# Expert gates of a decoder step scattered by matmuls: three bfloat16 parts in place of one float32 product, scaled on VectorE

## The chip, the core and the metric

The kernel runs on one core of a Trainium2 chip. The core has engines that run side by side and wait for each other by semaphores: TensorE (PE in the rows; PEld is its weight load), VectorE (DVE), ScalarE (ACT), GpSimd (POOL) and SyncE (SP). Each works through its own instructions in the order in which they stand. TensorE reads its operands from the on-chip memory SBUF and adds up its products in PSUM. The metric is the device time of one execution in microseconds; lower is better.

## The reference, cut to what matters

One step of a decoder layer: differential attention and a gated linear attention side by side, cross attention, and last a feed-forward layer of 16384 single-neuron experts, of which each token uses 128 (8 heads times 16). The change lies in that layer.

```
def one(xt):
    ...
    top_s, j = lax.top_k(cand_s, PEER_TOPK)
    e = jnp.take_along_axis(cand_i, j, axis=-1).reshape(blk, -1)
    g = jax.nn.softmax(top_s, axis=-1).reshape(blk, -1)
    act = jax.nn.gelu(jnp.einsum('ted,td->te', u[e], xt).astype(jnp.float32))
    return jnp.einsum('te,ted->td', (g * act).astype(xt.dtype), v[e])
```

There are 1024 prompt tokens (tiles 0 to 7 of 128) and 64 sample tokens (tile S). `e` is the expert's number, `g` its gate.

## The kernel before, in words

**Two ways to the experts.** For some tokens (`GORDER`) the kernel fetches the rows of `u` and `v` that they chose, one indirect DMA on POOL for each of 128 places (line 1232), and DVE makes a dot product (line 1238) or an accumulation (line 1245) of each: 640 of either. For the other 448 tokens (`DENSE`: half of tile 2 and tiles 3, 4, 5) it computes all 16384 experts with matmuls (`dense`, lines 1303 to 1370) and multiplies by a gate that is zero where an expert wasn't chosen. That needs the gates of a token as a 128 by 128 matrix W, where expert `e` stands in row `e >> 7` and column `e & 127`.

**How W is made.** `gates` (lines 1262 to 1301) runs once for each of the four tiles. It loads `e` and `g`, takes `e` apart, and transposes all three on TensorE, so that a token is a column and its 128 choices lie on the partitions. Then it goes through the tokens in 14 groups of 32 and, within a group, four times 8 tokens, 56 steps in all. In a step DVE compares a table of numbers `io8` with the row numbers of 8 tokens (`oa`, line 1288) and with their column numbers (`eb`, line 1289): one-hot rows, 128 wide, with the 8 tokens innermost. ACT multiplies `eb` by the gates, token by token (`ob`, 8 instructions, line 1291). TensorE forms `oa` transposed times `ob` for each token (line 1295), which adds each gate into its place; `oa` and `ob` are float32 here, and the operands of one token are 8 elements apart in memory. The profile shows a float32 matmul as two instructions. ACT copies the sums out of PSUM (line 1297), and SP stores a group to `Wd` in DRAM (line 1300). `oa`, `eb` and `ob` have two buffers each.

**What runs beside it.** `drive` (line 1481) steps the last post pass (tiles 6 and 7: output projection, cross attention, expert query, expert selection) and `gates` in turns, by the costs that they yield. In the rows, the post pass's matmuls are `accP` (lines 286 to 288), its weight splitting is `ws` (272 on ACT, 273 on DVE), and its selections are many small DVE instructions (lines 1014 to 1072, among them `eq`, line 1052, and `oh`, line 1055). A gather step is let in between (`paced`, line 1447). Its instructions are queued behind the instruction that `gmark` names on that instruction's engine; `gates` sets `gmark` to its scalings.

**What sets the order.** A scheduler with a timeline of its own orders the instructions of each engine, within the dependences and priorities. The dense stage follows: it loads `xs`, transposes it to `xTd` (lines 1310, 264, 246), then runs over blocks of 8 times 128 experts: scores `S` (line 1323), gelu and multiplication by W (`hx`, lines 1327 to 1334, which give `H`), and output `po` (line 1353).

Of the kernel before, what the change touches and what calls it, by code (L numbers as in the profile page):

```python
# [7 lines left out]
F32 = mybir.dt.float32  # L8
F32R = mybir.dt.float32r
BF = mybir.dt.bfloat16  # L10
I32 = mybir.dt.int32
U32 = mybir.dt.uint32
AF = mybir.ActivationFunctionType
OP = mybir.AluOpType
AX = mybir.AxisListType

P = 128
# [88 lines left out]
def step_kernel(ctx: ExitStack, tc: tile.TileContext, consts, a, outs):  # L106
    nc = tc.nc
# [3 lines left out]
    def mkpool(name, side="left"):  # L111
        return tc.tile_pool(name=name, bufs=1, side=side, reuse_waits="tile")
# [15 lines left out]
    def bank(tag):  # L128
        pool, n = banks[tag]
        return pool.tile([P, 512], F32, tag=tag, name=tag, bufs=n)  # L130
# [1131 lines left out]
    def gates(wp, t, io8):  # L1262

        e = wp.tile([P, P], I32, tag="we", name="we", bufs=1)
        nc.sync.dma_start(out=e, in_=eD[t * P:(t + 1) * P])
        ab = wp.tile([P, 2, P], I32, tag="wab", name="wab", bufs=1)
        nc.vector.tensor_scalar(ab[:, 0], e, 7, None, op0=OP.logical_shift_right)
        nc.vector.tensor_scalar(ab[:, 1], e, 127, None, op0=OP.bitwise_and)
        abg = wp.tile([P, 3, P], F32, tag="wf", name="wf", bufs=1)
        nc.vector.tensor_copy(abg[:, :2], ab)  # L1270
        nc.sync.dma_start(out=abg[:, 2], in_=gD[t * P:(t + 1) * P])
        pt = bank("wb").rearrange("p (j n) -> p j n", n=P)
        for j in range(3):
            nc.tensor.transpose(out=pt[:, j], in_=abg[:, j], identity=ident)
        T = wp.tile([P, 2, P], BF, tag="wT", name="wT", bufs=2)
        nc.vector.tensor_copy(T, pt[:, :2])
        tg = wp.tile([P, P], F32, tag="wm", name="wm", bufs=2)
        nc.vector.tensor_copy(tg, pt[:, 2])
        for g in range(4):
            if (t, g) not in goff:  # L1280
                continue
            st = wp.tile([P, 32, 4, 32], F32, tag="wst", name="wst", bufs=2)
            for q in range(4):
                c = slice(32 * g + 8 * q, 32 * g + 8 * q + 8)
                oa = wp.tile([P, P, 8], F32, tag="woa", name="woa", bufs=2)
                eb = wp.tile([P, P, 8], BF, tag="web", name="web", bufs=2)
                ob = wp.tile([P, P, 8], F32, tag="wob", name="wob", bufs=2)
                nc.vector.tensor_tensor(oa, io8, T[:, 0, c].unsqueeze(1).broadcast_to([P, P, 8]), op=OP.is_equal)
                nc.vector.tensor_tensor(eb, io8, T[:, 1, c].unsqueeze(1).broadcast_to([P, P, 8]), op=OP.is_equal)
                for k in range(8):  # L1290
                    gmark[0] = nc.scalar.activation(ob[:, :, k], eb[:, :, k], AF.Copy, scale=tg[:, c.start + k:c.start + k + 1]).ins
                for q4 in range(2):
                    ps = bank("wb").rearrange("p (t b) -> p t b", b=P)
                    for k in range(4):
                        nc.tensor.matmul(ps[:, k], lhsT=oa[:, :, 4 * q4 + k], rhs=ob[:, :, 4 * q4 + k], start=True, stop=True)  # L1295
                    o = 8 * q + 4 * q4
                    nc.scalar.copy(st[:, :, :, o:o + 4].rearrange("p g b t -> p (g b) t"),  # L1297
                                   ps.rearrange("p t b -> p b t"))
                yield 2.5
            nc.sync.dma_start(out=Wd[:, :, goff[t, g]].rearrange("g a x -> a g x"),  # L1300
                              in_=st.rearrange("p g b t -> p g (b t)"))
# [150 lines left out]
    gmark = [None]  # L1452
# [69 lines left out]
    op = ops.enter_context(mkpool("omg"))  # L1522
# [10 lines left out]
    while True:  # L1533
        c = next(m2)
# [31 lines left out]
    def all_gates(ts):  # L1566
        for t, _, _ in ts:
            yield from gates(gp, t, io8)
# [48 lines left out]
```

## Time and profile before

| | us |
|---|---|
| median of three runs | 4846.96 |
| lowest and highest of them | 4844.46 and 4854.68 |
| the profiled execution | 4846.62 |
| its span, first to last instruction | 4844.8 |

The profile is of one execution. Its busy time is a union of an engine's instructions; the same engine can be the limit in one stretch and idle in the next, so the stretches are to be read one by one. A wait is put down to what ended it. The granted clock of TensorE is a share of its full 2.4 GHz. The stages here, in us from the span's start: one-hot stage with post pass from 2975 to 3290, the rest of the post pass's selections up to about 3463, the dense stage's start beside and behind them, and the dense stage proper from about 3600 to the end.

### The profile page before, as it was taken

The page shows a single profiled execution, that of the slowest core. Times are in us where ns is not written, and L with a number is a line of the kernel's source. Part 1 is how long each engine was busy: PE and PEld are TensorE (multiplying, and loading weights), DVE is VectorE, ACT ScalarE, POOL GpSimd, SP SyncE. Part 2 cuts the span into 40 slices and gives each one's busy share as a digit, 9 for nine tenths or more (in the row PEclk, how much of TensorE's full clock was granted, in tenths as well). Part 3 has the DMA queues.
Part 4 walks back from the last instruction along what each step waited for, and adds up shares of the span by engine and source line. Part 5 has one row for each costly group of instructions (what it writes and reads, how often), then busy time and mean ns, then how long its engine had stood idle before and what let it go on. Part 6 is the DMA issues. An engine that isn't in the chain of part 4 may idle for free.

```text
span 4844.8 us, 74087 instructions
## 1 busy us (share of the span) xinstructions
PE 4003.1 (83%) x23952; PEld 3106.8 (64%) x23952; DVE 3626.2 (75%) x7813; ACT 2188.8 (45%) x4874; POOL 1742.3 (36%) x1509
## 2 busy tenths in 40 slices
PE   7987999789886776378678537997289999999999
PEld 5654666455554454256345326896279999999998
DVE  4442336766766789978778998679888889888887
ACT  4565666556652534155433336993123323332332
POOL 2000000124334545345444534233345444444542
PEclk9999999899998888589889768897699999999999
DMA  6778888799998887588788657787789999999996
GB/s 187 245 249 272 308 285 293 252 326 350 347 342 287 290 271 247 168 276 282 267 281 282 205 161 240 253 262 256 233 303 343 350 328 345 336 340 332 338 346 237
DMA packets 574629, 1370.40 MB, mean 283 GB/s; under 512 B 66401, under 2 KB 131233, under 8 KB 573473
## 3 DMA queue, kind: packets, MB, share of 16 engines
q1 hardware_dynamic: 376128, 669.92, 40.9%
q0 software_dynamic: 184320, 671.17, 40.6%
q10 hardware_dynamic: 13792, 24.58, 1.4%
q8 instruction: 190, 3.11, 0.3%
q14 instruction: 199, 1.62, 0.1%
HBM read 1306.52 MB, written 58.39 MB: 282 GB/s over the span
## 4 chain that ended last, share of the span: by engine, by line
PE 47%; DMA 18%; DVE 17%; issue 7%; ACT 5%; POOL 3%; SPq 2%; DVEq 0%; ACTq 0%; POOLq 0%
PE po L1353 11%; PE S L1323 11%; DMA g<-in_peer_v,e 7%; DVE g L1238 4%; PE tk L761 3%; DMA kp<-in_cache_diff_k 3%; DVE acc L1245 3%; PE wb L1295 3%; PE pt L264 2%; DMA g<-in_peer_u,e 2%; PE acc L287 2%; PE acc L286 2%; PE acc L288 2%; PE px L806 2%; PE pS L767 2%
## 5 line engine op out<-in xcount | busy, mean ns | idle before, releaser
L1232 POOL DMA_INDIRECT g<-in_peer_u,e x640 | 757.0, 1183 | 1086.4 <-DVE dots L1238 705.8
L1232 POOL DMA_INDIRECT g<-in_peer_v,e x640 | 756.1, 1181 | 927.7 <-DVE acc L1245 563.8
L1245 DVE SCALAR_TENSOR_TENSOR acc<-g,dots,acc 128x1024 f32<-128x1024 f32 x640 | 820.2, 1282 | 143.8 <-DMA g<-in_peer_v,e 140.1
L1238 DVE CUSTOM_DVE_ANT_0 g<-g,xn 128x1024 f32<-128x1024 f32 x640 | 773.5, 1219 | 57.4 <-DMA g<-in_peer_u,e 54.7
L1353 PE MATMUL po<-H,ws 128*128 128x448 f32 x3072 | 679.9, 368 | 93.3 <-ACT H L1333 86.5
L1323 PE MATMUL S<-xTd,uT 128*128 128x448 f32 x3072 | 696.1, 371 | 16.0 <-DVE uT L246 11.6
L1353 PEld LDWEIGHTS po<-H,ws 128*128 128x128 f32 x3072 | 570.8, 189 | 139.6 <-ACT H L1333 88.4
L1323 PEld LDWEIGHTS S<-xTd,uT 128*128 128x128 f32 x3072 | 575.1, 189 | 66.6 <-DVE uT L246 14.5
L273 DVE TENSOR_TENSOR ws<-raw,ws 128x512 fp32r<-128x512 f32 x544 | 369.9, 689 | 169.6 <-ACT ws L272 158.0
L272 ACT CAST ws<-raw 128x512 fp32r<-128x512 f32 x544 | 332.3, 621 | 274.7 <-DMA raw<-in_peer_w_q 89.6
L761 PE MATMUL tk<-cst,kp 128*128 128x128 f32 x2048 | 365.3, 298 | 86.5 <-DMA kp<-in_cache_diff_k 73.0
L761 PEld LDWEIGHTS tk<-cst,kp 128*128 128x128 f32 x2048 | 247.5, 149 | 244.0 <-issue 118.1
L764 ACT COPY kt<-tk 128x512 f32<-128x512 f32 x512 | 285.6, 594 | 162.0 <-PE tk L761 156.6
L227 POOL TENSOR_TENSOR rs<-ms,nhalf 128x1 f32<-128x1 f32 (+8 forms) x78 | 123.3, 1582 | 495.7 <-DVE ms L225 411.0
L287 PE MATMUL acc<-ws,T 128*128 128x512 f32 x608 | 256.3, 422 | 23.4 <-DVE ws L273 21.7
L646 PE MATMUL acc<-kT,qz 128*128 128x512 f32 (+3 forms) x384 | 190.1, 604 | 96.9 <-ACT P L657 88.8
L1345 ACT CAST ws<-raw 128x512 fp32r<-128x512 f32 x256 | 155.5, 623 | 243.1 <-DMA raw<-in_peer_v 144.4
L287 PE MATMUL accP<-ws,T 128*128 128x512 f32 x480 | 224.2, 468 | 48.0 <-DVE ws L273 47.4
L286 PE MATMUL acc<-ws,T 128*128 128x512 f32 x608 | 229.7, 427 | 24.2 <-ACT ws L272 19.2
L288 PE MATMUL acc<-ws,T 128*128 128x512 f32 x608 | 246.1, 405 | 0.0
L1295 PE MATMUL wb<-wob,woa 128*128 128x128 f32 x896 | 232.0, 424 | 10.7 <-ACT wst L1297 6.3
L286 PE MATMUL accP<-ws,T 128*128 128x512 f32 x480 | 192.6, 458 | 53.5 <-ACT ws L272 41.2
(432 smaller groups left out, 7285.9 us busy)
## 6 DMA issues: line engine op xcount, KB each, us to landing
kp<-in_cache_diff_k SPq DMA_DIRECT2D x512, 256.0 KB
vp<-in_cache_diff_v SPq DMA_DIRECT2D x512, 256.0 KB
raw<-in_peer_v SPq DMA_DIRECT2D x256, 256.0 KB
u<-in_peer_u SPq DMA_DIRECT2D x128, 512.0 KB
raw<-in_w_in SPq DMA_DIRECT2D x192, 256.0 KB
raw<-in_peer_w_q SPq DMA_DIRECT2D x128, 256.0 KB
Wd<-wst SPq DMA_DIRECT2D x14, 2048.0 KB
W<-Wd SPq DMA_DIRECT2D x32, 896.0 KB
```

The source lines that it names most:

```text
L272: nc.scalar.copy(ws[:, 0, :w], raw)
L273: nc.vector.tensor_tensor(ws[:, 1, :w], raw, ws[:, 0, :w].bitcast(F32), op=OP.subtract)
L286: nc.tensor.matmul(o, lhsT=T[t][:, 0, k, :n], rhs=ws[:, 0, :w], start=(k == 0), stop=False)
L287: nc.tensor.matmul(o, lhsT=T[t][:, 0, k, :n], rhs=ws[:, 1, :w], start=False, stop=False)
L288: nc.tensor.matmul(o, lhsT=T[t][:, 1, k, :n], rhs=ws[:, 0, :w], start=False, stop=(k == 7))
L761: nc.tensor.transpose(out=pt[:, pg * P:(pg + 1) * P], in_=kp[pg][:, j * P:(j + 1) * P], identity=ident)
L1232: nc.gpsimd.indirect_dma_start(out=g, out_offset=None, in_=src, in_offset=bass.IndirectOffsetOnAxis(ap=e[:, s:s + 1], axis=0))
L1238: nc.vector.tensor_tensor_reduce(out=g, in0=g, in1=xn, op0=OP.mult, op1=OP.add, scale=1.0, scalar=0.0, accum_out=dots[:, s:s + 1])
L1245: nc.vector.scalar_tensor_tensor(acc, g, dots[:, s:s + 1], acc, op0=OP.mult, op1=OP.add)
L1295: nc.tensor.matmul(ps[:, k], lhsT=oa[:, :, 4 * q4 + k], rhs=ob[:, :, 4 * q4 + k], start=True, stop=True)
L1323: nc.tensor.matmul(ps, lhsT=uT[:, i, k], rhs=xT[:, j, k], start=(k + i + j == 0), stop=(k == 7 and j == 1))
L1353: nc.tensor.matmul(po, lhsT=V[n][:, j, c], rhs=H[n][:, i], start=(n + i + j == 0), stop=(n == 7 and i == 1))
```

## The change

The gates are split into three bfloat16 parts whose sum is the float32 value: the first is the rounded value, the second the rounded rest, the third what then is left. The one-hot rows `oa` become bfloat16. In place of 8 scalings on ACT one DVE instruction multiplies `eb` with all three parts for 8 tokens (3072 elements on a partition). A token takes three bfloat16 matmuls that add into the same place of PSUM, in place of one in float32. `gates` no longer sets `gmark`, which keeps what the post pass last put there. The line numbers behind it move by seven.

```
-        tg = wp.tile([P, P], F32, tag="wm", name="wm", bufs=2)
-        nc.vector.tensor_copy(tg, pt[:, 2])
+        tg = wp.tile([P, 3, P], BF, tag="wm", name="wm", bufs=2)
+        rest = wp.tile([P, 2, P], F32, tag="wr", name="wr", bufs=1)
+        nc.vector.tensor_copy(tg[:, 0], pt[:, 2])
+        nc.vector.tensor_tensor(rest[:, 0], pt[:, 2], tg[:, 0], op=OP.subtract)
+        nc.vector.tensor_copy(tg[:, 1], rest[:, 0])
+        nc.vector.tensor_tensor(rest[:, 1], rest[:, 0], tg[:, 1], op=OP.subtract)
+        nc.vector.tensor_copy(tg[:, 2], rest[:, 1])
...
-                oa = wp.tile([P, P, 8], F32, tag="woa", name="woa", bufs=2)
+                oa = wp.tile([P, P, 8], BF, tag="woa", name="woa", bufs=2)
                 eb = wp.tile([P, P, 8], BF, tag="web", name="web", bufs=2)
-                ob = wp.tile([P, P, 8], F32, tag="wob", name="wob", bufs=2)
+                ob = wp.tile([P, 3, P, 8], BF, tag="wob", name="wob", bufs=2)
...
-                for k in range(8):
-                    gmark[0] = nc.scalar.activation(ob[:, :, k], eb[:, :, k], AF.Copy, scale=tg[:, c.start + k:c.start + k + 1]).ins
+                nc.vector.tensor_tensor(ob, eb.unsqueeze(1).broadcast_to([P, 3, P, 8]),
+                                        tg[:, :, c].unsqueeze(2).broadcast_to([P, 3, P, 8]), op=OP.mult)
...
                     for k in range(4):
-                        nc.tensor.matmul(ps[:, k], lhsT=oa[:, :, 4 * q4 + k], rhs=ob[:, :, 4 * q4 + k], start=True, stop=True)
+                        for x in range(3):
+                            nc.tensor.matmul(ps[:, k], lhsT=oa[:, :, 4 * q4 + k], rhs=ob[:, x, :, 4 * q4 + k],
+                                             start=(x == 0), stop=(x == 2))
```

The scheduler's order moves with it. The first place is DVE's queue near the end of the one-hot stage. Before, `woa` and `web` stand among selections (`v16`, `cse`) and weight splits (`ws`) of the post pass:

```order
L1289 TENSOR_TENSOR web_36683<-io8_33307,wT_35730 128x1024
L1014 MAX v16_36478<-sb_36476 128x8 x4
L225 TENSOR_SCALAR ms_36548<-ss2_36545 128x2
L1017 MAX v16_36173<-tmp_36175 128x8
L1017 MAX v16_36173<-tmp_36181 128x8
L273 TENSOR_TENSOR ws_36744<-raw_36742,ws_36744 128x512
L1034 TENSOR_TENSOR cse_36116<-csrc_36111 128x4x16
L1288 TENSOR_TENSOR woa_36682<-io8_33307,wT_35730 128x1024
```

After, the last two products `wob` of the stage are DVE's, and no weight split of the post pass is left beside them; what follows is selections and dot products:

```order
L1293 TENSOR_TENSOR woa_37293<-io8_33307,wT_36105 128x1024
L1295 TENSOR_TENSOR wob_37261<-web_37260,wm_36107 128x3072
L1295 TENSOR_TENSOR wob_37295<-web_37294,wm_36107 128x3072
L1018 MAX_INDEX i16_37396<-v16_37395,tmp_37415 128x8
L1017 MAX tv_36298<-tmp50_37086 128x8
L1017 MAX tv_36298<-tmp50_37092 128x8
L1016 MATCH_REPLACE tmp_37485<-v16_37483,sb_37481 128x128
L1238 ISA g_35122,dots_33926<-g_35122,xn_33922 128x1024
```

The one-hot steps have moved back against the post pass: from among its weight splits to behind the last of them.

The second place is SP's queue of DMAs at the hand-over to the dense stage. Before, the last stores of W stand among the loads of the last expert-query weights, and the dense inputs `xs` come some way behind:

```order
L1300 DMA Wd<-wst 128x32x128
L280 DMA raw<-in_peer_w_q 128x512 x4
L1300 DMA Wd<-wst 128x32x128
L280 DMA raw<-in_peer_w_q 128x512 x3
L1310 DMA xs<-xnd 64x1024
L1310 DMA xs<-xnd 128x1024
L280 DMA raw<-in_peer_w_q 128x512 x2
L1342 DMA raw<-in_peer_v 128x512 x4
L1310 DMA xs<-xnd 128x1024
```

After, the query weights are all loaded before, and four stores stand in a row just ahead of `xs`:

```order
L280 DMA raw<-in_peer_w_q 128x512 x6
L1349 DMA raw<-in_peer_v 128x512
L1307 DMA Wd<-wst 128x32x128
L1349 DMA raw<-in_peer_v 128x512 x5
L1307 DMA Wd<-wst 128x32x128 x4
L1317 DMA xs<-xnd 64x1024
L1317 DMA xs<-xnd 128x1024 x3
L1325 DMA u<-in_peer_u 128x1024 x7
```

The stores of W have moved back against the loads of the post pass, and the dense inputs with them.

## Rows read from the trace of the kernel before

**Rows 1.** The page's head: span, then each engine's busy us, share and instructions.

```profile
span 4844.8 us, 74087 instructions
PE 4003.1 (83%) x23952; PEld 3106.8 (64%) x23952; DVE 3626.2 (75%) x7813; ACT 2188.8 (45%) x4874; POOL 1742.3 (36%) x1509
```

**Rows 2.** Busy time by stretch; columns are named in the first row.

```profile
core 0: us, PE busy (x) PEld busy (x) DVE busy (x) ACT busy (x) POOL busy (x), PEclk, DMA share, GB/s
2700.00:2800.00 100.00, 35.97 (x123) 23.66 (x122) 98.19 (x347) 25.98 (x69) 52.52 (x34) 0.63 0.61 191
2800.00:2900.00 100.00, 40.19 (x132) 28.23 (x131) 99.22 (x349) 34.63 (x70) 33.83 (x24) 0.64 0.50 156
...
3800.00:4700.00 900.00, 900.00 (x4745) 830.70 (x4744) 791.66 (x1126) 274.16 (x511) 440.63 (x371) 1.00 0.93 339
...
2975.00:3290.00 315.00, 302.71 (x1301) 284.77 (x1300) 235.73 (x413) 286.62 (x661) 87.71 (x75) 0.93 0.79 255
3290.00:3463.00 173.00, 69.21 (x310) 55.27 (x309) 168.58 (x513) 39.19 (x95) 58.66 (x52) 0.65 0.73 235
...
2975.00:3463.00 488.00, 371.92 (x1610) 340.04 (x1608) 404.31 (x926) 325.81 (x754) 146.37 (x127) 0.83 0.77 248
```

**Rows 3.** DVE's waits from 2975 to 3463: us in total, times, longest.

```profile
DVE woa L1288 <- PE wb L1295: 40.9, 35, 2.9
DVE web L1289 <- ACT wob L1291: 12.0, 15, 2.7
DVE wT L1276 <- PE wb L1274: 10.7, 3, 7.8
DVE ws L273 <- ACT ws L272: 7.8, 4, 4.0
DVE acc L1245 <- DMA g<-in_peer_v,e: 4.8, 3, 3.2
```

**Rows 4.** Groups by line and shape, 2960 to 3300: busy us, mean ns, idle before.

```profile
L1295 PE MATMUL wb<-wob,woa 128*128 128x128 f32 x896 | 232.0, 424 | 10.7 <-ACT wst L1297 6.3 <-ACT wob L1291 4.4
...
L1291 ACT ACTIVATE wob<-web,wm 128x128 f32<-128x128 bf16 x448 | 198.5, 551 | 13.1 <-DVE web L1289 10.9 <-PE wb L1295 2.2
L1288 DVE TENSOR_TENSOR woa<-io,wT 128x1024 f32<-128x1024 bf16 x56 | 68.4, 1224 | 41.0 <-PE wb L1295 40.9
L1297 ACT COPY wst<-wb 128x512 f32<-128x512 f32 x112 | 63.7, 594 | 16.0 <-PE wb L1295 15.8
...
L1289 DVE TENSOR_TENSOR web<-io,wT 128x1024 bf16<-128x1024 bf16 x56 | 38.2, 685 | 12.0 <-ACT wob L1291 12.0
...
L1146 DVE TENSOR_TENSOR h<-accP,h 128x512 f32<-128x512 f32 x4 | 2.6, 684 | 0.4 <-PE accP L288 0.4
...
L1278 DVE COPY wm<-wb 128x128 f32<-128x128 f32 x4 | 1.1, 281 | 0.0
...
L1052 DVE TENSOR_TENSOR eq<-io,tjf 128x800 bf16<-128x800 bf16 x2 | 1.1, 570 | 0.0
```

**Rows 5.** Single lines: durations in ns (min/median/max), first and last start in us.

```profile
L1295 PEld LDWEIGHTS wb<-wob,woa x896: 312/337/340, 2975.9 to 3286.4; 128*128 128x128 f32 x180
...
L918 PE MATMUL accP<-cPT,mv x192: 272/275/583, 1686.6 to 3047.5; 128*128 128x128 f32 x192
...
L1291 ACT ACTIVATE wob<-web,wm x448: 509/542/694, 2973.5 to 3283.7; 128x128 f32<-128x128 bf16 x150
...
L1300 SPq DMA_DIRECT2D Wd<-wst x14: 360/377/426, 2996.1 to 3287.7; - x14
...
L264 PE MATMUL pt<-cst,xs x32: 311/421/477, 3324.8 to 3339.1; 128*128 128x128 f32 x24, 64*128 64x64 f32 x8
L1310 SPq DMA_DIRECT2D xs<-xnd x4: 326/388/577, 3296.4 to 3330.9; - x4
...
L246 DVE TENSOR_TENSOR xTd<-pt,xTd x8: 415/678/695, 3329.2 to 3345.3; 128x512 fp32r<-128x512 f32 x6, 128x256 fp32r<-128x256 f32 x2
...
L1055 DVE TENSOR_TENSOR oh<-eq,cse x72: 1547/1595/1743, 816.0 to 3463.3; 128x800 f32<-128x800 bf16 x64, 64x800 f32<-64x800 bf16 x8
```

**Rows 6.** Timeline of TensorE: start us, length us, instruction, how many in a row.

```profile
3001.73 1.39 PE L918 MATMUL accP<-cPT,mv 128*128 128x128 f32 x11
...
3218.16 0.40 PE L287 MATMUL accP<-ws,T 128*128 128x512 f32 x1
...
3218.39 0.40 PE L288 MATMUL accP<-ws,T 128*128 128x512 f32 x1
3218.39 2.00 PEld L1295 LDWEIGHTS wb<-wob,woa 128*128 128x128 f32 x8
```

**Rows 7.** The dense stage's last matmuls and the last gathers, as rows 5.

```profile
L1353 PE MATMUL po<-H,ws x3072: 358/363/740, 3474.8 to 4833.0; 128*128 128x448 f32 x192
...
L1232 POOL DMA_INDIRECT g<-in_peer_v,e x640: 932/950/6698, 1470.7 to 4796.8; - x160
```

**Rows 8.** TensorE's longest wait from 3463 to 3800, as rows 3.

```profile
PE po L1353 <- ACT H L1333: 85.9, 2, 85.3
```

## The prediction

> **What bounds the kernel now.** I read the page's head first, then busy time by stretch, then who waits for whom in the stretch that the change touches, then single lines. The head says TensorE (PE) is busy 83% and VectorE (DVE) 75% [rows 1]; both are averages over stages with different limits, so the stretches count. The one-hot stage runs from 2975 to about 3290: its matmuls (L1295) are all there, PE is busy 302.7 of 315 us, ScalarE (ACT) 286.6, DVE only 235.7 [rows 2, 5]. PE and ACT pace it, DVE has 79 us spare. From 3290 to 3463, where the last expert selection ends (last L1055 [rows 5]), it is the other way round: DVE 168.6 of 173, PE 69.2. The post pass for tiles 6 and 7 runs beside the one-hot stage, and its selections are what DVE is left with when PE lets go. Then the dense stage: PE is 900 of 900 us busy from 3800 to 4700 [rows 2], its last matmul starts at 4833.0 and the last expert gather at 4796.8 [rows 7]. So the end moves by what the dense stage's start moves, and that start is held by DVE: PE waits 85.3 us in one piece for H, whose DVE step stands behind the selections [rows 8]. The question is when DVE gets through its queue from 2975 to the last selection: 488 us now, 404.3 of them busy, 83.7 idle [rows 2].
>
> What the idle time waits for [rows 3]: 40.9 us the one-hot rows oa for PE to let go of their buffer, 12.0 us eb for ACT to let go of its, 10.7 us the transposed gates that stand behind the matmul backlog on PE; together 63.6 us that PE's and ACT's load causes. The other 20.1 us are casts, gathers and the like.
>
> **The change part by part, by engine.**
>
> ACT loses 448 scalings of 0.551 us [rows 4], some 245 us, and keeps the 112 copies out of PSUM. ACT is not a bound afterwards: 286.6 less about 200 in the same 315 us.
>
> PE: 448 tokens now cost two matmul instructions each (896 [rows 4]). Eight weight loads in 2.00 us, one lasting 0.337, are one each 0.238 us [rows 5, 6]; so 0.48 us a token, 213 us. After it there are three bfloat16 instructions a token, 1344. No row has this form with a step between elements. Below, one cannot be cheaper than a quarter of a 512-column float32r matmul (0.23 us from start to start [rows 6], so 0.058): 77 us. Above, nothing makes it dearer than the strided float32 instruction of now (0.238): 320 us. I take half of that, 0.119, because packed float32 instructions of the same shape start every 0.11 us (11 in 1.39 us, one lasting 0.275 [rows 5, 6]), twice the float32r price per column, and so half should be bfloat16's share of the strided price too: 160 us. PE then has about 250 of these 315 us and fits under DVE.
>
> A rule speaks against that middle value. Strided float32 operands cost 0.238 here against 0.11 packed [rows 5, 6]. The Trainium skill (SBUF — State Buffer, section "Door 1: The DMA port swizzle") says that SBUF has lines of 16 bytes, that each access on a new line pays, and that one strides for free as far as 8 bfloat16 or 4 float32. The step goes from 32 bytes to 16. By the rule's last half PE would pay the packed price, the 77 us above (an estimate), and the last rival below would be dead; by its first half it would pay at least the 160, and that rival keeps its chance. The float32 rows agree that 32 bytes cost; no row here shows 16.
>
> DVE gains work. L1289, all bfloat16, takes 0.685 us for 1024 elements, L1052 0.570 for 800: 0.513 ns an element. L1288, which writes float32, takes 1.224 [rows 4]. The rows oa become bfloat16 and fall to 0.685: 56 x 0.539 = 30.2 us less. The scaled rows are 56 products of 3072 elements, all bfloat16: 0.685 + 2048 x 0.000513 = 1.736 us, 97.2 us in all. Were this form to run an element at a time, the slope would be that between L1146 (512 elements, 0.684) and L1288: 1.055 ns, so 3.38 us each, 189 us. I take the fast one: L1289 has the same types and the same repeated inner row of eight. Splitting the gates is five small instructions for one, four times, at L1278's 0.281 or a little less: +4 us. Neighbours on DVE overlap by 0.09 us, so 60 more instructions cost 5 us less than their sum. Net: 97 - 30 + 4 - 5 = 66 us more.
>
> Orders: in the scheduler's order 384 of the 640 dot products and 347 accumulations stand ahead of the last selection, against 384 and 349 before; so the gathers bring DVE nothing new there. That the gates no longer set the mark behind which gathers are queued moves only a few gathers on GpSimd (POOL); I cost it at nothing, since gathers end 36 us before the last matmul [rows 7], and that slack is what it would eat first. The 14 stores of W keep their size.
>
> **The sum.** DVE work from 2975 to the last selection: 404.3 + 66 = 470 us. Idle time: PE's and ACT's 63.6 us go, 20.1 stay. 470 + 20 = 490, against 488. So what PE and ACT lose, DVE takes up; the dense stage starts 2 us later, and from there nothing changes. The profiled execution took 4846.62 us (span 4844.8); 4849 is the forecast. The median of the three runs is 4846.96, so this is no change: a measurement of this kernel tells about 0.2%, 9.7 us, from none.
>
> **The rivals.**
>
> Faster, by better filling. Where DVE paced the kernel before with projections, selections and gathers beside each other (2700 to 2900), it was busy 98.2 and 99.2 of 100 us [rows 2]. At 98.5% the 470 us take 477: 11 us less, 4836, and with no idle time at all 18 less, 4829. For it: ACT, now at 91%, is nearly free, so casts come sooner. Against it: the first hundred microseconds hold cross attention and the loading of four gate tiles, chains between engines that DVE waits through in its strict order.
>
> Slower, at the hand-over to the dense stage. The dense inputs xs may be loaded only behind the last stores of W on SP's queue. Before, 45 us pass from the last scaled row (3283.7) over the last store (3287.7), the first xs load (3296.4) and its transposes (3324.8) to the first DVE step on it (3329.2) [rows 5], and DVE has selections to do meanwhile. After it the one-hot stage runs on almost to the end of the selections: the last four stores stand in a row just ahead of xs, and only 56 DVE instructions (75 as the profile counts them) lie between the last product and the first step on xs; at 168.6 / 513 = 0.33 us each [rows 2] that is 25 us. If the chain still takes 45, DVE stands still for 20 us with every selection behind it: 4869. It decides as soon as the chain takes longer than 25 us. Against it: part of the 45 was PE's backlog, which shrinks; store and load alone took some 13 us until the load was issued.
>
> Slower, because the product doesn't run packed: 189 instead of 97 us, so 4941. The same types in L1289 speak against it.
>
> Slower, because PE stays the bound: strided bfloat16 as dear as strided float32, 320 us instead of 213. Over 2975 to 3463 PE would then have 371.9 + 107 = 479 us of work beside DVE's 470, each waiting for the other in turn: some 30 to 90 us more, 4877 to 4937. At the lower of PE's two clock levels the middle price would double to the same figure; PE's granted clock was 0.63 of full where DVE paced [rows 2]. For it speaks only that no row shows the form.
>
> **How the numbers follow.** Forecast (DVE takes over with the idle time that I leave it): 0.41. Better filling: 0.26. Hand-over: 0.25. No packing: 0.04. PE still the bound: 0.04. The first is within 0.2%, the second faster, the last three slower: faster 0.26, same 0.41, slower 0.33. The range goes from 4826, a little under the case of no idle time, to 4885, past the hand-over and the lower edge of a PE bound; what is left out is the 0.04 without packing, most of PE's and a few hundredths at either end. The forecast's own range is 4837 to 4857.
>
> **What would show it.** Right: DVE at 95% or more from 2975 to the last selection, that selection within 10 us of 3463, the waits for wb and wob gone from DVE's list, the product near 1.74 us, PE clearly under DVE in that stretch. Hand-over: DVE idle in one piece just ahead of the first step on xTd. Wrong altogether: a last selection before 3440, which would mean that DVE work I count was cheaper or moved behind it; a dense stage that no longer runs PE at 100%; or a product of 3.4 us.

## The result and the profile after

The changed kernel takes 4965.91 us (median of 4 runs, 4961.08 to 4974.5) against 4850.52 us for the kernel before (4844.46 to 4854.68): a ratio of 1.0243, 95% interval 1.0229 to 1.0257. It is 115 us slower. The forecast was 4849, with a range of 4826 to 4885: the time lies outside, and on the side that had a chance of 0.33, in a case that had 0.04.

The profiled execution has a span of 4961.4 us. First the page's head, then busy time by stretch in the columns of [rows 2]:

```profile
span 4961.4 us, 74540 instructions
PE 4128.7 (83%) x24400; PEld 3107.5 (63%) x24400; DVE 3693.0 (74%) x7885; ACT 2010.5 (41%) x4426; POOL 1753.7 (35%) x1509
...
2975.00:3290.00 315.00, 298.23 (x1195) 203.47 (x1194) 208.95 (x319) 82.11 (x161) 65.59 (x54) 0.69 0.58 184
2975.00:3580.00 605.00, 501.98 (x2056) 342.42 (x2054) 469.67 (x995) 149.12 (x309) 157.15 (x125) 0.65 0.62 198
3380.00:3481.00 101.00, 81.18 (x343) 49.17 (x342) 97.31 (x239) 18.26 (x39) 33.93 (x25) 0.50 0.64 196
...
3900.00:4800.00 900.00, 900.00 (x4748) 833.12 (x4747) 787.33 (x1134) 272.04 (x508) 437.39 (x369) 1.00 0.94 337
```

PE's share in the head is that of before and DVE's one point lower [rows 1]; the head hides the loss. The stretches show it: ACT has fallen from 286.6 to 82.1 us in 2975 to 3290, PE has stayed at 298, and DVE has not gained there, it has lost, 209.0 against 235.7 [rows 2]. The dense stage is as full as before, 900 of 900. Now the changed lines, one by one (ns min/median/max, first and last start):

```profile
L1301 PEld LDWEIGHTS <-woa x1344: 141/145/172, 2975.4 to 3481.1; 128*128 128x128 bf16 x192
L1301 PE MATMUL wb<-wob,woa x1344: 388/414/451, 2982.3 to 3481.4; 128*128 128x128 bf16 x192
...
L1295 DVE TENSOR_TENSOR wob<-web,wm x56: 1743/1753/1764, 2980.5 to 3470.2; 128x3072 bf16<-128x3072 bf16 x56
...
L1055 DVE TENSOR_TENSOR oh<-eq,cse x72: 1551/1594/1760, 804.2 to 3579.2; 128x800 f32<-128x800 bf16 x64, 64x800 f32<-64x800 bf16 x8
...
L1360 PE MATMUL po<-H,ws x3072: 358/363/743, 3588.6 to 4949.6; 128*128 128x448 f32 x192
```

The last one-hot matmul starts at 3481.4, before at 3286.6; the last selection starts at 3579.2, not 3463.3 [rows 5], 115.9 us later; the last dense matmul starts at 4949.6, not 4833.0 [rows 7], 116.6 later. The whole loss is made before the last selection and then handed on unchanged. What DVE and PE waited for in 2975 to 3580, as [rows 3]:

```profile
DVE woa L1293 <- PE wb L1301: 97.7, 34, 8.2
DVE wT L1276 <- PE wb L1274: 12.5, 3, 5.6
...
PE wb L1301 <- DVE wob L1295: 41.8, 11, 10.8
...
ACT wst L1304 <- PE wb L1301: 305.6, 107, 7.5
```

The wait of the one-hot rows for PE was meant to vanish; it went from 40.9 us [rows 3] to 97.7, and 96.0 of these lie before 3380: up to there PE is what the others wait for. From 3380 to the last one-hot matmul DVE is busy 97.3 of 101 us and PE waits for its products.

The price of one matmul is read from the timeline (start, length, instruction, how many in a row):

```profile
3047.98 11.43 PE L1301 MATMUL wb<-wob,woa 128*128 128x128 bf16 x48 [4.36 <-DVE wob L1295]
3104.47 5.82 PE L1301 MATMUL wb<-wob,woa 128*128 128x128 bf16 x24
```

From start to start that is (11.43 - 0.414) / 47 = 0.234 us in the first run, which lies at the lower of the two granted clocks (0.50) but for its first microsecond, and (5.82 - 0.414) / 23 = 0.235 us in the second, at the higher (1.00). Over all 1344 the median is 234 ns at either clock. The prediction had taken 119.

### The profile page after: what moved, and what is told of

It is laid out like the page before. It is cut to its first block, busy times and chain, and to the rows that moved or that the text cites. A ratio compares the mean times of both kernels' runs of the same rounds, so it can differ in the third digit from the quotient of the medians.

```text
span 4961.4 us, 74540 instructions
## 1 busy us (share of the span) xinstructions
PE 4128.7 (83%) x24400; PEld 3107.5 (63%) x24400; DVE 3693.0 (74%) x7885; ACT 2010.5 (41%) x4426; POOL 1753.7 (35%) x1509
## 4 chain that ended last, share of the span: by engine, by line
PE 49%; DMA 18%; DVE 18%; issue 7%; ACT 3%; POOL 3%; SPq 2%; DVEq 0%; POOLq 0%; ACTq 0%
PE po L1360 11%; PE S L1330 10%; DMA g<-in_peer_v,e 8%; PE wb L1301 5%; DVE g L1238 3%; DMA kp<-in_cache_diff_k 3%; DVE acc L1245 3%; PE tk L761 3%; PE pt L264 2%; PE acc L287 2%; PE acc L286 2%; POOL g L1232 2%; PE acc L288 2%; DMA g<-in_peer_u,e 2%; PE px L806 2%
## 5 line engine op out<-in xcount | busy, mean ns | idle before, releaser
L1232 POOL DMA_INDIRECT g<-in_peer_v,e x640 | 766.9, 1198 | 1002.1 <-DVE acc L1245 651.4
L1301 PE MATMUL wb<-wob,woa 128*128 128x128 bf16 x1344 | 322.0, 415 | 41.8 <-DVE wob L1295 41.8
L1301 PEld LDWEIGHTS <-woa 128*128 128x128 bf16 x1344 | 193.2, 146 | 164.9 <-DVE wob L1295 29.8
L287 PE MATMUL acc<-ws,T 128*128 128x512 f32 x608 | 259.7, 428 | 20.7 <-DVE ws L273 20.3
L287 PE MATMUL accP<-ws,T 128*128 128x512 f32 x480 | 230.2, 480 | 44.0 <-DVE ws L273 43.3
L286 PE MATMUL acc<-ws,T 128*128 128x512 f32 x608 | 230.6, 429 | 27.9 <-ACT ws L272 24.0
L288 PE MATMUL acc<-ws,T 128*128 128x512 f32 x608 | 248.9, 410 | 0.0
```

Of the source, the lines that this page charges most:

```text
L286: nc.tensor.matmul(o, lhsT=T[t][:, 0, k, :n], rhs=ws[:, 0, :w], start=(k == 0), stop=False)
L287: nc.tensor.matmul(o, lhsT=T[t][:, 0, k, :n], rhs=ws[:, 1, :w], start=False, stop=False)
L288: nc.tensor.matmul(o, lhsT=T[t][:, 1, k, :n], rhs=ws[:, 0, :w], start=False, stop=(k == 7))
L1232: nc.gpsimd.indirect_dma_start(out=g, out_offset=None, in_=src, in_offset=bass.IndirectOffsetOnAxis(ap=e[:, s:s + 1], axis=0))
```

## The experiments

**The theory** formed from these rows: a matmul's price is set by the distance in bytes between successive elements of its moving operand (`rhs`, here wob; `lhsT`, here woa, are its weights), not by its type; from 16 bytes on each element is paid for by itself. An operand whose elements are neighbours is called packed. **Rivals**: the distance in the weights costs it; three products that add up in one place, or three times as many weight loads, cost it; the product on DVE or the hand-over to the dense stage costs it; the price is one of float32 against bfloat16. All kernels but e8, where VectorE has two more instructions per eight tokens and the scheduler's order shifts with them, keep the instruction order of the one that they are made from. Ratios are to the kernel before in the same set of runs (medians of 4845.13 to 4852.65). Of e4, e5, e6 and e8 the profiled execution lies 10, 30, 16 and 8 us below the median of the runs, of e3 16 us above; times are judged by the medians, the rows explain them. Executions also reach the one-hot stage at different times, up to 21 us apart, with the same instructions ahead of it in the same order. So the stage is best measured from its own first instruction. From the first woa to the last selection it takes 493 us before (2970.5 to 3463.3) and 607 after (2972.1 to 3579.2).

### e1: the moving rows read as neighbours

```diff
- rhs=ob[:, x, :, 4 * q4 + k]
+ rhs=ob.rearrange("p x b t -> p x (b t)")[:, x, (4 * q4 + k) * P:(4 * q4 + k + 1) * P]
```

> The changed kernel, in which the matmuls read their moving operand (the scaled rows) as 128 neighbouring elements instead of elements 8 apart (16 bytes); every other instruction and its order stay. What is multiplied is then not what the reference asks for: the gates' places are mixed up, so it is run for its time. Theory A (the step between elements of the moving operand costs 0.234 us a matmul whatever the clock): the 1344 matmuls fall to between 0.06 and 0.12 us from start to start, VectorE paces the stage, the last selection comes near 3465 to 3480 and the time near 4849 to 4865. Theory B (three products that add up in one place of PSUM, or three times as many weight loads, cost it): the matmuls stay at 0.234 us and the time near 4966.

Measured: 4852.0 us, ratio 0.9996 (0.9983 to 1.0009). One changed operand gives the whole loss back. Its matmuls at the higher clock and at the lower one, its stretch from 2975 to the last selection, its product, its last selection, and DVE's wait for PE:

```profile
3059.59 1.71 PE L1301 MATMUL wb<-wob,woa 128*128 128x128 bf16 x24
3100.49 2.78 PE L1301 MATMUL wb<-wob,woa 128*128 128x128 bf16 x24 [5.11 <-DVE wob L1295]
...
2975.00:3473.00 498.00, 284.53 (x2081) 241.78 (x2080) 474.08 (x1018) 151.69 (x315) 189.72 (x130) 0.74 0.76 247
...
L1295 DVE TENSOR_TENSOR wob<-web,wm 128x3072 bf16<-128x3072 bf16 x56 | 97.4, 1748 | 0.0
...
L1055 DVE TENSOR_TENSOR oh<-eq,cse x72: 1547/1593/1737, 808.2 to 3473.0; 128x800 f32<-128x800 bf16 x64, 64x800 f32<-64x800 bf16 x8
...
DVE woa L1293 <- PE wb L1301: 5.4, 1, 5.4
```

A matmul takes 62 ns at the higher and 107 at the lower clock. DVE is busy 474 of 498 us (the forecast's sum was 470 busy and 20 idle). The last selection comes 10 us after that of before, but the stage began 12 us later: from its first woa (2982.7) it takes 490 us for 493. So everything but the matmul's price went as the prediction had it. The rivals on DVE and the hand-over fall, and so does that on the three products and their weight loads, which are all still there.

### e2: the weights read as neighbours

```diff
- lhsT=oa[:, :, 4 * q4 + k]
+ lhsT=oa.rearrange("p b t -> p (b t)")[:, (4 * q4 + k) * P:(4 * q4 + k + 1) * P]
```

> The changed kernel, in which the matmuls read their weights (the one-hot rows oa) as 128 neighbouring elements, while the moving operand keeps its step of 8 elements; order the same, the gates again mixed up, run for its time. Theory A: the weight load lies hidden under the matmul; it may get shorter than 0.145 us, but the matmuls stay at 0.234 us from start to start and the time at 4966 within 10. Theory C (the weights' step is what costs): matmuls at 0.06 to 0.12 us and a time near 4850.

Measured (one run): 4969.76 us, a matmul 227 ns. The weight load did get shorter, 126 ns for 145, but the matmul's price did not follow:

```profile
L1301 PEld LDWEIGHTS <-woa x1344: 95/126/152, 2989.2 to 3486.6; 128*128 128x128 bf16 x192
L1301 PE MATMUL wb<-wob,woa x1344: 386/405/432, 2995.2 to 3486.9; 128*128 128x128 bf16 x192
```

The rival on the weights falls.

### e3 and e7: the moving rows 8 and 4 bytes apart

```diff
- rhs=ob[:, x, :, 4 * q4 + k]
+ rhs=ob.rearrange("p x b t -> p x (b t)").rearrange("p x (h b t) -> p x h b t", h=2, t=4)[:, x, q4, :, k]
```

> The changed kernel, in which the moving operand is read with a step of 4 elements (8 bytes) instead of 8 (16 bytes); order the same, the gates mixed up, run for its time. If two elements in a line of 16 bytes are enough for the full rate: as with packed rows, matmuls at 0.06 to 0.12 us, time 4849 to 4865. If the price goes with the distance: about 0.12 us, time within 15 us of that all the same, since TensorE is then not the bound. If any step costs the same: 0.234 us and 4966.

> The changed kernel with the moving operand of the 1344 matmuls read with a step of 2 elements (4 bytes) instead of 8; gates and tokens are thereby mixed up, so only its time counts. A price of 1.83 ns for each 16-byte line that the operand touches gives 32 lines, 59 ns, which is below what a packed matmul took (62 ns at full clock, 107 at low): the matmul then takes 62 to 107 ns, as packed, and the time is 4850 to 4855. A price for any step other than 1 gives 122 ns, as with a step of 4, and 4856.

Measured: e3 4856.38 us, ratio 1.0009 (0.9997 to 1.0021), a matmul 122 ns at either clock; e7, the same in steps of 2 (one run), 4856.06 us, a matmul 63 ns at the higher and 107 at the lower clock, as packed in e1. A run of 24 of e7, then one of 48 of e3:

```profile
3057.11 1.74 PE L1301 MATMUL wb<-wob,woa 128*128 128x128 bf16 x24
...
3013.23 6.00 PE L1301 MATMUL wb<-wob,woa 128*128 128x128 bf16 x48
```

16 bytes 234, 8 bytes 122, 4 bytes no more than packed. 234 / 128 = 1.83 ns for every 16 bytes in which an element of the operand lies gives 234, 117 and 59 ns; within 5 ns of what was measured where it is above the packed rate. So the price falls with the number of elements that share 16 bytes until it meets that rate. It is not a price for any step above 1. Whether it is paid by the 16 bytes that are touched, or by the distance up to 16 bytes, no run separates: for the distances here the two come to the same. The Trainium skill (SBUF — State Buffer, "Door 1: The DMA port swizzle") counts in the same 16-byte lines, and its first half, that each access on a new line pays, fits these rows. Its second half, that one strides for free as far as 8 bfloat16 or 4 float32, does not hold for the moving operand: 8 bfloat16 cost 234 ns for 62 (e1), 4 cost 122, and 4 float32 cost 234 for 112 (e4 and e5 below).

### e4: float32 rows 16 bytes apart

The kernel before, with 4 tokens innermost instead of 8 in woa, web, wob and io8.

```diff
- ob = wp.tile([P, P, 8], F32, tag="wob", name="wob", bufs=2)
+ ob = wp.tile([P, 2, P, 4], F32, tag="wob", name="wob", bufs=2)
...
- nc.tensor.matmul(ps[:, k], lhsT=oa[:, :, 4 * q4 + k], rhs=ob[:, :, 4 * q4 + k], start=True, stop=True)
+ nc.tensor.matmul(ps[:, k], lhsT=oa[:, q4, :, k], rhs=ob[:, q4, :, k], start=True, stop=True)
```

> The kernel before with its float32 operands laid out for 4 tokens instead of 8 innermost, so that elements of a token lie 16 bytes apart instead of 32; the same sums, the same order. Theory A says that the step costs in float32 too: if 16 bytes are cheaper than 32, the matmul instruction falls from 0.238 towards 0.11 us; TensorE then has some 200 us in place of 303 in the one-hot stage, ScalarE (287 us busy) paces it, and the time falls by 10 to 40 us, to 4810 to 4837. If 16 bytes cost as much as 32: matmuls 0.238 us, time 4847 within 10.

Measured: 4829.58 us, ratio 0.9961 (0.9946 to 0.9977). The matmul stayed at 234 ns (240 before), so 16 bytes are as dear as 32 and the type is not what counts. The stage takes 473 us for 493. What changed most is ACT, which writes wob and reads web: it has 516 ns a scaling instead of 551 [rows 4], and DVE's wait for it is 1.3 us instead of 12.0 [rows 3]. That this made the gain is argued, since the matmul, too, has fallen by 6 ns. The rows of e4, of 2975 to 3290 and 2975 to 3463:

```profile
L1291 ACT ACTIVATE wob<-web,wm 128x128 f32<-128x128 bf16 x428 | 142.1, 516 | 11.1 <-DVE web L1289 6.9 <-PE wb L1295 4.2
...
DVE woa L1288 <- PE wb L1295: 32.8, 29, 2.9
DVE web L1289 <- ACT wob L1291: 1.3, 2, 1.1
```

### e5, e6, e9 and e10: float32, token by token

e5 is the kernel before with both operands stored token by token; e6 adds 4 tokens innermost in web; e9 adds that DVE writes woa in its own order; e10 is the kernel before with woa alone as in e9.

```diff
- oa = wp.tile([P, P, 8], F32, tag="woa", name="woa", bufs=2)
- ob = wp.tile([P, P, 8], F32, tag="wob", name="wob", bufs=2)
+ oa = wp.tile([P, 8, P], F32, tag="woa", name="woa", bufs=2)
+ ob = wp.tile([P, 8, P], F32, tag="wob", name="wob", bufs=2)
...
- nc.scalar.activation(ob[:, :, k], eb[:, :, k], AF.Copy, ...)
+ nc.scalar.activation(ob[:, k], eb[:, :, k], AF.Copy, ...)                # e5
+ nc.scalar.activation(ob[:, k], eb[:, k // 4, :, k % 4], AF.Copy, ...)    # e6, e9
...
+ nc.vector.tensor_tensor(oa.rearrange("p t b -> p b t"), io8, ...)        # e5; e6 alike
+ nc.vector.tensor_tensor(oa, iotab.unsqueeze(1).broadcast_to([P, 8, P]),  # e9, e10
+     T[:, 0, c].unsqueeze(2).broadcast_to([P, 8, P]), op=OP.is_equal)
```

> The kernel before with its float32 selectors and rows stored token by token, so that both operands of each of the 896 matmuls are 128 neighbouring float32 elements (before: 32 bytes apart); VectorE writes woa and ScalarE writes wob in that layout, ScalarE still reads web with a step of 8 tokens. Theory (the moving operand's distance sets the matmul's cost; what lies in one 16-byte line is paid once): a matmul takes 0.11 us from start to start instead of 0.234, TensorE loses about 896 x 0.12 = 107 us of its work between 2975 and 3463, and then ScalarE and VectorE decide; VectorE was busy 404 us there in the kernel before, so the last selection comes at some 3400 to 3420 and the time is 4790 to 4815. Rival (float32 products cost the same in any layout, and the gain of the run with 4 tokens innermost came from ScalarE alone): a matmul stays at 0.23, and the time is that run's, 4830, or, if ScalarE still pays for its step of 8, 4850.

> As the run with float32 rows token by token, and with web and the index row io8 stored with 4 tokens innermost, so that ScalarE reads its 128 elements 8 bytes apart instead of 16. Theory: ScalarE's scaling falls as in the run with 4 tokens innermost or further (551 to 516 ns or less), TensorE's as in the run beside it, and the time is 0 to 15 us below that run's. Rival (ScalarE's scaling is paid by its write alone, and writing neighbouring elements has already brought it): the same time as the run beside it, within 4 us.

Measured: e5 4835.0 us, ratio 0.9966 (0.995 to 0.9982); e6 4817.84, 0.993 (0.9906 to 0.9953). The matmul fell to 112 ns at the higher clock as the theory said, yet e5's time is 20 us above what was expected. Its profiled execution, at 4805.63 us, is within that range, but it came to the stage 21 us early. Here are the first and last woa of before and of e5, the last selection of e5, and its rows by line and shape, 2975 to 3290:

```profile
L1288 DVE TENSOR_TENSOR woa<-io,wT x56: 1212/1225/1268, 2970.5 to 3276.0; 128x1024 f32<-128x1024 bf16 x56
...
L1288 DVE TENSOR_TENSOR woa<-io,wT x56: 1885/1960/2036, 2949.6 to 3239.8; 128x1024 f32<-128x1024 bf16 x56
L1055 DVE TENSOR_TENSOR oh<-eq,cse x72: 1549/1592/1812, 802.9 to 3425.8; 128x800 f32<-128x800 bf16 x64, 64x800 f32<-64x800 bf16 x8
...
L1288 DVE TENSOR_TENSOR woa<-io,wT 128x1024 f32<-128x1024 bf16 x50 | 98.1, 1965 | 5.7 <-PE wb L1295 5.7
...
L1291 ACT ACTIVATE wob<-web,wm 128x128 f32<-128x128 bf16 x409 | 180.4, 582 | 9.6 <-DVE web L1289 9.5
```

So the stage takes 476 us in e5, 17 fewer than before, as the medians have it (18). What PE saved by reading neighbours, DVE paid in good part by writing woa 512 bytes apart: 1965 ns for 1224 [rows 4]. And ACT, which still read web 16 bytes apart, got slower, not faster (582 ns for 551), though it now wrote neighbours; it did get faster in e6, where web's distance is 8 bytes and the scaling takes 404 ns. So e6's second expectation (the write alone counts) fell, and the time followed by 17 us, a little over the 15 expected; the stage takes 461 us.

> As the run with float32 operands token by token and web with 4 tokens innermost, but VectorE writes woa in its own order (token by token, neighbouring elements), with the token's row number as the operand that is repeated along the row. There woa took 1965 ns, in the kernel before, with 8 tokens innermost, 1225. Theory (the 1965 ns are the writes 512 bytes apart): woa falls to 1.1 to 1.25 us, VectorE, which is the bound in that run's stage (453 of 488 us busy), loses 56 x 0.74 = 41 us, TensorE's wait for woa (23.7 us) goes, and the last selection and the time come 15 to 40 us earlier: 4780 to 4805. Rival (a repeated operand along the row slows VectorE as much as the strided write): woa stays near 2 us and the time within 5 us of that run's, 4818.

Measured: 4798.21 us, ratio 0.991 (0.989 to 0.9931). woa takes 1217 ns, DVE's wait for PE to free woa is down to 1.8 us, the stage takes 440 us for 493, and the last selection comes at 3414.3, 49.0 us before that of [rows 5]; the last dense matmul starts at 4783.0, 50.0 before that of [rows 7]. It is the fastest of all the kernels here.

```profile
2975.00:3290.00 315.00, 244.91 (x1430) 207.29 (x1430) 283.19 (x584) 250.67 (x711) 131.51 (x93) 0.90 0.92 301
...
L1295 PE MATMUL wb<-wob,woa x896: 270/275/582, 2977.9 to 3237.6; 128*128 128x128 f32 x180
...
L1288 DVE TENSOR_TENSOR woa<-iotab,wT x56: 1198/1216/1271, 2974.4 to 3225.9; 128x1024 f32<-128x1024 bf16 x56
L1291 ACT ACTIVATE wob<-web,wm x448: 389/411/463, 2977.4 to 3235.1; 128x128 f32<-128x128 bf16 x150
...
L1055 DVE TENSOR_TENSOR oh<-eq,cse x72: 1532/1600/1757, 810.4 to 3414.3; 128x800 f32<-128x800 bf16 x64, 64x800 f32<-64x800 bf16 x8
```

> The kernel before with only woa, the weights of the 896 float32 matmuls, stored token by token (written so by VectorE); the moving rows wob stay 32 bytes apart. Theory (only the moving operand's distance counts): a matmul still takes 0.23 us from start to start, and the time stays within 10 us of 4850. Rival (in float32 the weights' layout carries part of the gain seen with both operands packed, 0.11 us): the matmul falls to 0.11 to 0.18, and the time by 20 us or more.

Measured (one run): 4841.65 us; the matmul stayed at 233 ns at the higher and 236 at the lower clock. In float32 too it is the moving operand alone.

### e8: the change with 2 tokens innermost

```diff
- ob = wp.tile([P, 3, P, 8], BF, tag="wob", name="wob", bufs=2)
+ ob = wp.tile([P, 3, 4, P, 2], BF, tag="wob", name="wob", bufs=2)
...
- rhs=ob[:, x, :, 4 * q4 + k]
+ rhs=ob[:, x, 2 * q4 + k // 2, :, k % 2]
```

> The change as it stands (bfloat16 rows and selectors, three products per token), but with 2 tokens innermost instead of 8 in woa, web, wob and io8, so that a matmul's rows lie 4 bytes apart; VectorE makes the scaled rows in three instructions of 1024 elements instead of one of 3072. Theory (distance of the moving operand is what cost the 115 us): a matmul takes 62 to 107 ns; if VectorE keeps its speed with runs of 2, the three products take 1.75 to 1.9 us together and the time is 4850 to 4860, level with the kernel before, with VectorE as the bound. Rival (VectorE's doubled speed needs the run of 8): 3 x 1.1 = 3.3 us, 56 x 1.5 = 84 us more, and 4930 to 4945.

Measured: 4849.03 us, ratio 0.9992 (0.9976 to 1.0008): level with the kernel before. DVE keeps its speed with runs of 2 (681 ns for each third of the product), and it is the bound:

```profile
2975.00:3463.00 488.00, 273.01 (x2043) 223.36 (x2042) 468.17 (x1096) 149.54 (x308) 178.29 (x126) 0.75 0.76 244
...
L1296 DVE TENSOR_TENSOR wob<-web,wm 128x1024 bf16<-128x1024 bf16 x164 | 103.4, 681 | 0.0
```

So the idea behind the change, bfloat16 parts, is worth nothing here even when the layout is mended: it moves some 65 us of work onto DVE (469.7 busy for 404.3), which was the next bound. Mending the layout of the float32 kernel (e9) is worth 47 us.

### The prices side by side

Median ns from start to start of one matmul instruction, 128 x 128, counted from the traces:

| type | distance of moving elements | higher clock | lower clock | kernel |
|---|---|---|---|---|
| bfloat16 | 16 bytes | 234 | 234 | after |
| bfloat16 | 16 bytes, weights packed | 227 | 227 | e2 |
| bfloat16 | 8 bytes | 122 | 122 | e3 |
| bfloat16 | 4 bytes | 63 | 107 | e7 |
| bfloat16 | 4 bytes, weights 4 bytes | 57 | 107 | e8 |
| bfloat16 | neighbours | 62 | 107 | e1 |
| float32 | 32 bytes | 240 | 240 | before |
| float32 | 32 bytes, weights packed | 233 | 236 | e10 |
| float32 | 16 bytes | 234 | 236 | e4 |
| float32 | neighbours | 112 | 213 | e5, e6, e9 |

## Why the prediction was wrong

**What bounds the kernel: right.** The end moved by what the last selection moved, 115.9 and 116.6 us here, 49.0 and 50.0 in e9; the dense stage stayed full.

**ACT: right.** The scalings went and ACT waits 305.6 us for PE.

**PE: the step that failed.** The prediction took 119 ns a matmul, 160 us, between bounds of 77 and 320 us. Measured: 234 ns; 1344 x 0.234 = 314 us, next to the upper bound of 320. The argument for the middle was that bfloat16 should cost half of float32 strided because float32 packed costs twice the float32r price per column. That took the strided price for a multiple of the packed one. It is a price of its own: it doesn't depend on the type (234 and 234 at 16 bytes, e4) and hardly on the clock, so the prediction's doubling at the lower clock did not come either (122 at both in e3); and it replaces the packed rate where it is the higher. The rows had a hint: 0.238 a strided float32 instruction, 0.11 a packed one [rows 5, 6], is a factor that nothing explained; scaling an unexplained price by the type was the error. With no row between bounds as far apart as 77 and 320 us, the rival at the upper one deserved far more than 0.04.

**DVE: right.** The product took 1753 ns (1736 forecast), woa 690 (685). From 2975 to the last selection DVE was busy 469.7 us of 605, where the sum said 470. What missed was idle time: 135 us for 20, and 97.7 + 12.5 us of it wait for PE. With PE's price mended (e1) it is 474 busy and 24 idle.

**The rule that was weighed.** The prediction set the rule of the Trainium skill (SBUF — State Buffer, "Door 1: The DMA port swizzle") beside the trace and left it open. Its first half is what happened, and the prediction ran it at "at least the 160" instead of one full price per element, 320.

**The rivals.** PE as the bound (0.04) is what happened, but its own time, 4877 to 4937, was too low by 29 us or more. It reckoned with 479 us of PE work; the trace has 502 us busy to 3580. Counted from start to start, from 2965 to the last selection and without the idle gaps, PE has 381 us before and 509 after: 98 of the difference on L1295/L1301, 18 on the post pass's matmuls at L286 to L288, 12 on the rest. Those 30 us on instructions that the change doesn't touch go with the granted clock, which was 0.69 in 2975 to 3290 where it had been 0.93 [rows 2]: L287 takes 566 ns on average after the change and 480 before (groups by line and shape, 2975 to 3580 of after, then 2975 to 3463 of before).

```profile
L287 PE MATMUL accP<-ws,T 128*128 128x512 f32 x96 | 54.3, 566 | 0.0
...
L287 PE MATMUL accP<-ws,T 128*128 128x512 f32 x96 | 46.1, 480 | 4.1 <-DVE ws L273 4.1
```

What PE did before the clock fell can be read from the trace: a run of one-hot matmuls without a gap, the post pass's matmuls ahead of it and behind it, and the stretch of the run in two parts:

```profile
3068.70 0.39 PE L286 MATMUL accP<-ws,T 128*128 128x512 f32 x1
3068.94 8.62 PE L1301 MATMUL wb<-wob,woa 128*128 128x128 bf16 x36
...
3077.78 0.63 PE L288 MATMUL accP<-ws,T 128*128 128x512 f32 x1
...
3080.25 0.39 PE L288 MATMUL accP<-ws,T 128*128 128x512 f32 x1
...
3068.94:3073.00 4.06, 4.06 (x19) 2.60 (x19) 1.00 (x2) 0.59 (x1) 1.14 (x1) 0.97 0.67 212
3073.00:3077.00 4.00, 4.00 (x19) 2.48 (x18) 0.00 (x0) 0.00 (x0) 0.00 (x0) 0.50 0.14 51
```

The clock fell to its lower level (1.2 of 2.4 GHz) inside the run, though PE was never idle, and rose again behind it, when the post pass's matmuls had run for a while. From 2975 to 3290 it fell 18 times, 16 of them so; with packed rows (e1) it fell 14 times there, each time behind idle time of PE. So what filled PE with strided bfloat16 matmuls also slowed its neighbours. No run sets the clock by itself, so the 30 us are an account, not an experiment. The hand-over (0.25) did not come: in e1, where DVE paces, the last product started at 3367.8 and the first step on xTd at 3390.4, a chain of 22.6 us under the 25 us of work that DVE has there, and DVE waited 1.1 us in all from 3340 to 3473. Better filling (0.26) did not come either in e1 or e8 by more than the measurement tells (stages of 490 and 493 us for 493). No packing (0.04) was rightly small.

## What to carry to other kernels

Before a strided operand is given to TensorE, look in the trace for one matmul of the same size with packed operands: if the strided one is dearer, the distance sets its price, and here a narrower type at the same count of elements per 16 bytes bought nothing. Choose the tile's inner axis for all who touch it: here 2 tokens innermost kept DVE's speed in bfloat16 and TensorE's packed rate, and in float32 token by token did, once DVE wrote in that order too. Measure a stage from its own first instruction before two executions are set side by side. And where one price decides which engine is the bound and no row shows it, give the bound that hurts its own chance.

## What the runs showed of the hardware

- A moving operand costs TensorE 1.83 ns for each 16 bytes that hold an element of it for 128 elements (234 ns at 16 bytes, 240 at 32, 122 at 8), in either type at 16 bytes (8 were run in bfloat16 alone) and at either clock; from 4 bytes down the packed rate holds (62 ns bfloat16, 112 float32 at the higher clock).
- The weights' distance hardly counts: 227 for 234 ns (e2), 233 for 240 (e10), and 57 for 63 beside moving elements 4 bytes apart (e8, e7), though the load itself gets shorter (126 for 145 ns in e2).
- ACT, too, pays for distance: a scaling took 582 ns reading bfloat16 16 bytes apart and 404 reading 8 bytes apart, both writing neighbours (e5, e6).
- DVE writing float32 512 bytes apart took 1965 ns for 1024 elements, 1217 in its own order (e6, e9); an operand repeated along the row cost it nothing there (1224 before).
- A run of strided bfloat16 matmuls without a gap took the granted clock from 1.00 to 0.50 within it; the matmuls behind it took 0.63 us for 0.39 until it rose again (after, 3068 to 3080).
